# Column dots of a diffusion-transformer layer: where the unused products are written, and new tables for the order of the work

## The chip, the cores and the metric

The kernel runs on one core of a Trainium2 chip, which works with five engines that run side by side, each through its own list of instructions in order: TensorE (PE; PEld is its loading of weights), VectorE (DVE), ScalarE (ACT), GpSimd (POOL) and SyncE (SP). SyncE only starts transfers (DMA) here. The metric is the device time of one launch in microseconds, as a median of several runs.

## The reference

One step of a transformer layer for two groups of 128 tokens (a prompt and a sample), all in float32, with D_MODEL = 2048:

```python
sh1, sc1, g1, sh2, sc2, g2 = split(silu(cond) @ w_ada + b_ada, 6)
h = rms_norm(x, norm1_w) * (1 + sc1) + sh1
qa, ka, va, qb, kb, vb, ga, gb = split(h @ w_in)            # 2048 x 8704
oa = window_attention(qa, ka, va, cache_a, sink)
ob = neighbourhood_attention(qb, kb, vb, cache_b, rpb)
x = x + g1 * ((sigmoid(ga) * (oa @ w_br_a) + sigmoid(gb) * (ob @ w_br_b)) @ w_out)
h2 = rms_norm(x, norm2_w) * (1 + sc2) + sh2
x = x + g2 * (square(relu(h2 @ w_up)) @ w_down)             # 2048 x 8192, 8192 x 2048
```

Here `cond` is one vector for each group, so `silu(cond) @ w_ada` is a product of two rows with a matrix of 2048 x 12288. The outputs are the two results x and the normalised keys and the values of both attentions for the prompt.

## The kernel before

**Weight steps.** The large products are walked through in 456 weight steps, one after another: w_in first (the first 72 steps, then the two gates up to step 135), then the two branch products (136 to 167), w_out (168 to 199), the first part of w_up (200 to 215), and then in turn eight groups of 16 steps of w_down and seven of w_up. A step takes a weight tile of 128x1024 float32 (`raw`, 512 KB, loaded by SyncE) and does 12 matmuls of 128x512. Each float32 product is made of three products of fp32r numbers: the weight is split into a high part `wH`, a copy that ScalarE makes (`copy`, line 103), and a low part `wL` = `raw` - `wH`, which VectorE makes (line 265); the activations are split in the same way (`hH`, `hL`). The three products are wH x hH, wL x hH and wH x hL (lines 323 to 325, 434 to 436). For the steps listed in `LO_DMA`, ScalarE writes -wH (line 271) and a transfer started by GpSimd adds the raw weight to it in place (line 272). In the seven late w_up groups a pair of tiles is combined as in fast matrix multiplication, with further tiles `t` (line 1361), `tH`, `tL`, `uH`, `uL` (line 1373), `XH`, `XL` and `YB`, which VectorE and ScalarE make, and with accumulators `Q` (lines 1295 to 1297).

**The order of the work.** It is written out by hand, and no scheduler changes it: the function `run` walks the steps, and at each step it issues, to all engines, the loads that are due, the high and the low parts that are due, the step's matmuls and then the side work that is listed for this step. How far ahead these are is a matter of tables with one digit for each step: `RUN` (loads), `HIA` (high parts) and `LOOK` (low parts). Other tables name the steps at which side work is issued: `POST` and `JOBS` (attention), `U_AT`, `M_AT`, `P_UP`, `STAT_AT`, `XS_AT`, `CONST_AT`, `ADA_AT`, `ROW_AT`, and, for the dots below, `DOTS1`, `DOTS` and `DOTS2`. The tiles `raw`, `wH`, `wL`, `aT` and most others come from one pool of 54 buffers of 4 KB a partition, each reused when its last reader is done. Some accumulators are seeded: `seed` copies earlier sums into the two PSUM banks on ScalarE (line 103, `acc<-u_kvA` or `acc<-dsum`), so that the step's first matmul must wait for it.

**The column dots.** Most of `silu(cond) @ w_ada` isn't done on TensorE. A tile `aT` of 128x1024 transposed weights is loaded by SyncE (`dot_load`), and for each of the two condition vectors (s = 0 and 1), which lie in `cB` on all partitions, VectorE multiplies the tile with the vector and sums along the row (`dot`, line 1522). The sums go into a column; the products themselves are written somewhere and never read. There are 144 such tiles and so 288 dots. The tables list the step of a tile's first dot; the second is issued one step later. For s = 0 the products go into `junk`, a uint8 tile of which there is one buffer; for s = 1 they go over `aT` itself. Two instructions of VectorE that write the same place are kept in order by a wait of the second one for the first.

The second part of the layer begins with a norm: the residual sums (lines 1067, 1068), square sums on ScalarE (line 1072), a power on GpSimd (line 149), and the scaled rows `h2f` (line 1145), which TensorE transposes (line 1153).

Of the kernel before, what the change touches and what calls it, by code (L numbers as in the profile page):

```python
# [18 lines left out]
P = 128  # L19
# [13 lines left out]
FB_DVE = 0  # L33
FB1 = 12
H_AT = 41
DOTS1 = [16, 17, 17, 19, 21, 27, 28, 32, 33, 34, 34, 38, 38, 38, 40, 40]
CHUNKS = [2, 2, 2, 4, 6]
NFAST = 8
FAST = {1: (0, 1, 2, 3, 4, 5, 6, 7), 2: (0, 1, 2, 3, 4, 5, 6, 7), 3: (0, 1, 2, 3, 4, 5, 6, 7), 4: (0, 1, 2, 3, 4, 5, 6, 7), 5: (0, 1, 2, 3, 4, 5, 6, 7), 6: (0, 1, 2, 3, 4, 5, 6, 7), 7: (0, 1, 2, 3, 4, 5, 6, 7)}
# [14 lines left out]
LOOK = "320122121112425413003123131135113254310254350030712111112489598342112325488911310001241110220222620000300000133400492100202426272442137656655964688684888655653375207130430225548804351610138881841040342174117523461045214446120432245411630040106853042961221010000201202222102552542682111475746010001224011275268574765000072101111321216724428800000406300034322212447772056830563557354369716120300331113174563712714401401033133311121375789630000046530676935775"
RUN = "535358982521111211111000000030102324221111112122111110400652246572543003264232120122432752120112142152010012210035788736651103254942768867787999998987232212799999975115897587998887988775789998987770031443789698865239899876766555766886999623766758875434952511611133325753488988557066786888855675457768777795999985878788788878868488887888988699988672200555565048944929988999999987899999887876245789999999999384555456235656556714366470168961004152442522213555"
CONST_AT = [44, 56, 80, 86, 104, 86]
ADA_AT = [None, 5, 13, 20, 24, 38]
XS_AT = {1: 14, 2: 2, 3: 23}
POST = {('kvA', 0): [54, 57, 78], ('qA', 0): [54, 59, 66], ('qA', 1): [62, 70, 79], ('kB', 0): [71, 71, 79], ('qB', 0): [75, 82, 91], ('kB', 1): [89, 101, 104], ('qB', 1): [82, 87, 106]}
JOBS = [[81, 85, 87, 93, 102], [82, 84, 88, 97, 111], [80, 86, 97, 103, 112], [88, 98, 103, 109, 111], [103, 103, 106, 115, 122], [105, 105, 108, 109, 126], [108, 108, 119, 123, 126], [113, 114, 117, 121, 125]]  # L60
SS_AT = [74, 74, 128, 139]
T_AT = [3, 4]
PREP_IN = [5, 7]
DOTS = [46, 52, 53, 55, 56, 56, 57, 58, 61, 65, 65, 65, 68, 70, 70, 70, 70, 75, 75, 75, 77, 78, 79, 82, 84, 85, 87, 88, 89, 92, 92, 92, 94, 95, 95, 95, 101, 101, 101, 103, 104, 104, 107, 108, 108, 109, 110, 110, 110, 111, 112, 113, 117, 120, 120, 121, 123, 124, 124, 124, 132, 132, 132, 132, 132, 133, 133, 134, 140, 143, 143, 145, 145, 150, 150, 156, 156, 156, 156, 159, 162, 163, 171, 172, 173, 175, 179, 179, 186, 186, 186, 187, 188, 188, 189, 190]
DOTS2 = [235, 237, 238, 264, 269, 270, 301, 301, 330, 331, 333, 361, 367, 371, 393, 397, 424, 425, 428, 433, 433, 433, 433, 433, 439, 439, 441, 441, 441, 442, 444, 444]
STAT_AT = [2, 0, -1, 8]
U_AT = [[[3, 3, 3, 5, 9, 20, 20, 21, 22], [14, 14, 15, 15, 16, 20, 20, 30, 30]], [[2, 5, 5, 5, 16, 16, 18, 29, 29], [11, 13, 14, 14, 14, 26, 26, 27, 27]], [[9, 10, 10, 10, 11, 15, 29, 30, 30], [12, 17, 21, 21, 21, 29, 33, 33, 33]], [[4, 7, 7, 8, 9, 10, 11, 12, 13], [2, 3, 4, 4, 8, 9, 25, 29, 31]], [[0, 4, 4, 10, 10, 21, 21, 23, 24], [3, 3, 5, 5, 9, 24, 30, 31, 31]], [[3, 9, 9, 10, 10, 26, 28, 29, 29], [8, 10, 11, 12, 12, 21, 25, 32, 32]], [[0, 5, 9, 9, 9, 10, 12, 12, 13], [0, 0, 7, 7, 9, 13, 15, 16, 16]]]
XLO_IN = True
STAY = [(3, 1), (3, 2), (5, 2), (5, 3)]
TL_DMA = [2, 3]  # L70
M_TE = (3,)
M_AT = [2, 6, 10]
FLIP = 2
P_UP = [2, 0]
T_UP = [7, 17]
COL = {"qA": 0, "kvA": 1024, "qB": 1536, "kB": 2560, "vB": 3584, "gA": 4608, "gB": 6656}

# [2 lines left out]
def tile_hybrid_step(ctx: ExitStack, tc: tile.TileContext, a):  # L80
# [4 lines left out]
    sp = ctx.enter_context(tc.tile_pool(name="small", bufs=6))  # L85
# [204 lines left out]

    by_dma = sorted(LO_DMA)

    def run():
        loads.sort(key=lambda x: x[:2])
        for st in wsteps:
            while loads and loads[0][0] <= st["i"] + int(RUN[st["i"]]):
                loads.pop(0)[2]()
            for j in sorted(j for j in pre if j <= st["i"]):
                for fn in pre.pop(j):
                    fn()  # L300
            to = st["i"] + int(LOOK[st["i"]]) + 1
            while by_dma and by_dma[0] < to + LO_AHEAD:
# [704 lines left out]
    def br_unit(n):  # L1007
# [503 lines left out]
    def dot(box, job, second, s, tag):  # L1511

        which, fb = job
        if which == "g1":
            dst, part = gcol[which][:, s, fb:fb + 1], 2
        elif which == "g2":
            dst, part = g2col[fb // 4][:, s, fb % 4:fb % 4 + 1], 5
        else:
            nsub, w = which
            dst, part = mod[nsub][w][:, fb, s:s + 1], 3 * nsub + w  # L1520
        out = box["raw"] if s else sp.tile([P, 1024], mybir.dt.uint8, name="junk", tag="J", bufs=1)
        dve.tensor_tensor_reduce(out, box["raw"], cB[s, tag], 1.0, dst if second else baT[:, part, fb:fb + 1],  # L1522
                                 OP.mult, OP.add, dst)

# [94 lines left out]
    for c in range(FB_DVE // 2):  # L1619
        box = {}  # L1620
# [97 lines left out]
```

## Time and profile before

| | |
|---|---|
| median of 3 runs | 1298.91 us (1298.57 to 1299.99) |
| span of the profiled execution | 1296.4 us |
| VectorE, column dots, one each (line 1522) | 1.29 us |
| ScalarE, one copy of 128x1024 (line 103) | 1.04 us |
| transfers | 430.54 MB, mean 332 GB/s |

The profile is of one execution. The span runs from its first to its last instruction; the device time of that execution isn't given apart from the runs, and the median lies 2.5 us above the span. In rows of the profile, line numbers are those of the kernel, `out<-in` names the tiles, and a bracket at the end of a timeline row holds the time that the engine stood idle before it and what ended that. All times are in microseconds from the span's start.

### The profile page before, as it was taken

Reading aid. Unit: us, or ns where it says so; the run is one execution under the profiler, and the core shown is the slowest. Engines: PE = TensorE matmul, PEld = TensorE weight load, DVE = VectorE, ACT = ScalarE, POOL = GpSimd, SP = SyncE. Lnnn points to the kernel's source line nnn. Section 1 sums busy time; section 2 is a strip of 40 time slices with the busy share of each in tenths; the row PEclk is TensorE's granted clock in tenths of the full one; section 3 lists DMA queues with packets and bytes.
Section 4 is the critical chain, followed back from the end, with each engine's and each line's share of the span. In section 5 each row is a group of like instructions: output and inputs, shape, how many; then the busy total and the mean of one; then the engine's idle time right before and its main releaser. Section 6 shows DMA issues by size and latency. Waiting matters only on the chain.

```text
span 1296.4 us, 18038 instructions
## 1 busy us (share of the span) xinstructions
PE 1283.7 (99%) x6074; PEld 1043.7 (81%) x6074; DVE 1215.9 (94%) x1610; ACT 962.4 (74%) x1363; POOL 104.1 (8%) x129
## 2 busy tenths in 40 slices
PE   8999999999999999999999999999999999999998
PEld 4777788888878888888887888888888888888886
DVE  4599999999999999999889999999999999999997
ACT  5535779878676755746798798887899878899872
POOL 0000002121200000001101000100000000010010
PEclk9999999999999999999999999999999999999999
DMA  9999999999999999999799999899999989999995
GB/s 372 408 409 409 394 348 378 355 331 338 363 355 367 381 388 324 343 371 308 252 283 305 327 298 326 283 292 353 296 334 250 299 302 290 309 292 347 379 345 178
DMA packets 158428, 430.54 MB, mean 332 GB/s; under 512 B 53072, under 2 KB 54336, under 8 KB 158336
## 3 DMA queue, kind: packets, MB, share of 16 engines
q1 hardware_dynamic: 145264, 383.39, 80.2%
q0 software_dynamic: 12880, 45.91, 16.6%
q8 instruction: 47, 0.77, 0.2%
q14 instruction: 45, 0.37, 0.1%
q10 hardware_dynamic: 192, 0.10, 0.1%
HBM read 403.35 MB, written 14.99 MB: 323 GB/s over the span
## 4 chain that ended last, share of the span: by engine, by line
PE 80%; DVE 8%; DMA 5%; ACT 5%; issue 2%; POOL 0%; DVEq 0%; SPq 0%; ACTq 0%
PE acc L323 15%; PE acc L324 15%; PE acc L325 15%; PE Q L1296 5%; PE Q L1297 5%; PE Q L1295 5%; PE acc L434 5%; PE acc L436 5%; PE acc L435 5%; DVE wL L265 1%; DMA araw<-in_w_pair 1%; DVE aT L1522 1%; DVE junk L1522 1%; PE ps_ada L340 1%; DMA raw<-in_w_down 1%
## 5 line engine op out<-in xcount | busy, mean ns | idle before, releaser
L103 ACT ACTIVATE wH<-raw 128x1024 fp32r<-128x1024 f32 (+1 forms) x347 | 348.3, 1044 | 129.1 <-DMA raw<-in_w_in 39.5
L265 DVE TENSOR_TENSOR wL<-raw,wH 128x1024 fp32r<-128x1024 f32 x297 | 347.9, 1222 | 6.8 <-ACT wH L103 5.6
L434 PE MATMUL acc<-wH,hH 128*128 128x512 f32 x276 | 108.6, 393 | 0.0
L435 PE MATMUL acc<-wL,hH 128*128 128x512 f32 x276 | 107.5, 390 | 0.0
L436 PE MATMUL acc<-wH,hL 128*128 128x512 f32 x276 | 107.5, 390 | 0.0
L323 PE MATMUL acc<-wH,hH 128*128 128x512 f32 x256 | 102.9, 402 | 0.0
L324 PE MATMUL acc<-wL,hH 128*128 128x512 f32 x256 | 100.1, 391 | 0.3 <-DMA wL<-in_w_in 0.3
L325 PE MATMUL acc<-wH,hL 128*128 128x512 f32 x256 | 99.9, 390 | 0.0
L1522 DVE CUSTOM_DVE_ANT_0 junk<-aT,cB,cols 128x1024 uint8<-128x1024 f32 x72 | 92.6, 1286 | 0.7
L1522 DVE CUSTOM_DVE_ANT_0 aT<-aT,cB,cols 128x1024 f32<-128x1024 f32 x72 | 92.0, 1298 | 0.5
L1361 DVE TENSOR_TENSOR t<-raw 128x1024 f32<-128x1024 f32 x56 | 68.4, 1222 | 2.2 <-PE acc L324 1.3
L103 ACT ACTIVATE uH<-raw 128x1024 fp32r<-128x1024 f32 x56 | 58.9, 1051 | 14.6 <-DVE raw L1367 11.1
L1373 DVE TENSOR_TENSOR tL<-t,tH 128x1024 fp32r<-128x1024 f32 x56 | 68.4, 1222 | 1.0 <-ACT tH L103 0.9
L1373 DVE TENSOR_TENSOR uL<-raw,uH 128x1024 fp32r<-128x1024 f32 x56 | 68.4, 1222 | 0.2
L103 ACT ACTIVATE tH<-t 128x1024 fp32r<-128x1024 f32 x56 | 58.8, 1050 | 11.7 <-DVE t L1361 8.4
L103 ACT ACTIVATE XH<-raw 128x1024 fp32r<-128x1024 f32 x56 | 58.8, 1051 | 10.2 <-PE acc L324 5.3
L434 PEld LDWEIGHTS acc<-wH,hH 128*128 128x128 f32 x276 | 51.8, 188 | 12.4 <-issue 2.1
L436 PEld LDWEIGHTS acc<-wH,hL 128*128 128x128 f32 x276 | 51.8, 188 | 11.0
L435 PEld LDWEIGHTS acc<-wL,hH 128*128 128x128 f32 x276 | 51.8, 188 | 10.7 <-DVE wL L265 0.2
L324 PEld LDWEIGHTS acc<-wL,hH 128*128 128x128 f32 x256 | 48.1, 188 | 11.0 <-DMA wL<-in_w_in 0.9
L323 PEld LDWEIGHTS acc<-wH,hH 128*128 128x128 f32 x256 | 48.1, 188 | 10.0 <-issue 0.7
L325 PEld LDWEIGHTS acc<-wH,hL 128*128 128x128 f32 x256 | 48.1, 188 | 10.0
(668 smaller groups left out, 3468.3 us busy)
## 6 DMA issues: line engine op xcount, KB each, us to landing
raw<-in_w_in SPq DMA_DIRECT2D x133, 512.0 KB, 10.2
raw<-in_w_down SPq DMA_DIRECT2D x128, 512.0 KB, 10.2
raw<-in_w_upF SPq DMA_DIRECT2D x112, 512.0 KB, 6.6
aT<-in_w_adaT SPq DMA_DIRECT2D x80, 512.0 KB, 9.9
aT<-in_w_gT SPq DMA_DIRECT2D x64, 512.0 KB, 10.2
araw<-in_w_pair SPq DMA_DIRECT2D x48, 512.0 KB, 10.2
raw<-in_w_out SPq DMA_DIRECT2D x32, 512.0 KB, 10.1
XL<-in_w_upF POOLq DMA_DIRECT2D x21, 512.0 KB, 8.2
```

Source lines behind the costliest of these rows:

```text
L103: act.activation(out, in_, AF.Copy)
L265: dve.tensor_tensor(st["lo"], st["raw"], st["hi"].bitcast(F32), op=OP.subtract)
L323: pe.matmul(acc[tb], sh, wh[:, k, :], start=f, stop=False, **kw)
L324: pe.matmul(acc[tb], sh, wl[:, k, :], start=False, stop=False, **kw)
L325: pe.matmul(acc[tb], sl, wh[:, k, :], start=False, stop=l, **kw)
L434: pe.matmul(acc[tb], sh, wh[:, k, :], start=kt == 0 and k == 0 and not held and not seeded, stop=False, **kw)
L435: pe.matmul(acc[tb], sh, wl[:, k, :], start=False, stop=False, **kw)
L436: pe.matmul(acc[tb], sl, wh[:, k, :], start=False, stop=last and k == 1 and not hold, **kw)
L1295: pe.matmul(acc, stat[0], hi, start=f, stop=False)
L1361: dve.tensor_tensor(t.rearrange("p (a n) -> p a n", a=2), X.rearrange("p (a n) -> p a n", a=2), Y[:, 0:512].unsqueeze(1).to_broadcast([P, ...
L1373: dve.tensor_tensor(b[n + "L"], v, b[n + "H"].bitcast(F32), op=OP.subtract)
L1522: dve.tensor_tensor_reduce(out, box["raw"], cB[s, tag], 1.0, dst if second else baT[:, part, fb:fb + 1], OP.mult, OP.add, dst)
```

## The change

Line 1521 takes the place for the unused products from `junk` for both dots of a tile, and `junk` now has two buffers in turn. All tables of the side work, and the tables for loads, high parts and low parts, have new numbers. `LO_DMA` has 61 steps where it had 65; of the steps below 200 there are 24 in both. On average a high part is made 7.5 steps ahead of its use (6.4 before) and a low part 5 (4 before), as the order has it.

```diff
-DOTS1 = [16, 17, 17, 19, 21, 27, 28, 32, 33, 34, 34, 38, 38, 38, 40, 40]
+DOTS1 = [17, 18, 19, 20, 23, 27, 30, 32, 34, 34, 37, 37, 37, 38, 40, 40]
...
-HIA = "001212220310102113100001210001100012133414312347213667640200000004600001000320473311554222331525515435463425300014421235010000005113000005420012000010000
...
+HIA = "400113522030440010420200211110041100202342333511313676025142910360060641102322362041732050474443682205452062200032820224629062315003111414070500976030200
...
-ROW_AT = [5, 7, 9, 5]
+ROW_AT = [6, 6, 6, 4]
...
-CONST_AT = [44, 56, 80, 86, 104, 86]
-ADA_AT = [None, 5, 13, 20, 24, 38]
-XS_AT = {1: 14, 2: 2, 3: 23}
+CONST_AT = [48, 54, 79, 82, 103, 89]
+ADA_AT = [None, 5, 13, 21, 24, 38]
+XS_AT = {1: 4, 2: 2, 3: 24}
...
-STAT_AT = [2, 0, -1, 8]
+STAT_AT = [3, 0, -1, 8]
...
-M_AT = [2, 6, 10]
+M_AT = [4, 6, 8]
...
-P_UP = [2, 0]
+P_UP = [3, 1]
...
-        out = box["raw"] if s else sp.tile([P, 1024], mybir.dt.uint8, name="junk", tag="J", bufs=1)
+        out = sp.tile([P, 1024], mybir.dt.uint8, name="junk", tag="J", bufs=2)
```

`LO_DMA`, `LOOK`, `RUN`, `POST`, `JOBS`, `DOTS`, `DOTS2` and `U_AT` change in the same way. What the numbers do is seen in the order of the instructions, at three places.

The first is VectorE among the dots, where w_in is under way, with what each instruction waits for in brackets (DVE_49 is a wait for an earlier instruction of VectorE itself, DMAHW for a transfer; every dot has a second row, the read of its sum). Before:

```order
L1522 ISA junk,scT_158<-aT,cB_1202,cols 128x1024 [waits DMAHW1_49]
L1522 ISA scT_158 128x1
L1522 ISA junk,shT_157<-aT,cB_1202,cols 128x1024 [waits DMAHW2_49,DVE_49]
L1522 ISA shT_157 128x1
L1522 ISA junk,scT_158<-aT,cB_1202,cols 128x1024 [waits DVE_49]
L1522 ISA scT_158 128x1
L1522 ISA aT,scT_158<-aT,cB_1204,cols 128x1024
```

And of the change:

```order
L1522 ISA junk,scT_158<-aT,cB_1085,cols 128x1024
L1522 ISA scT_158 128x1
L1522 ISA junk,shT_157<-aT,cB_1083,cols 128x1024 [waits DMAHW0_49]
L1522 ISA shT_157 128x1
L265 TENSOR_TENSOR wL<-raw,wH 128x1024 [waits DMAHW1_49,DMASW1_49,PE_49]
L265 TENSOR_TENSOR wL<-raw,wH 128x1024 [waits DMAHW6_49,Activation_49]
L1522 ISA junk,shT_157<-aT,cB_1085,cols 128x1024 [waits DVE_49]
```

Before, the second and third dot into `junk` each wait for the dot directly ahead of them. Of the change, the two dots that follow each other write into two buffers and have no such wait, and where a dot waits for VectorE, the instruction that it waits for is at least two dots back. Of the 288 dots, 72 waited for the instruction directly ahead before, and none does now.

The second is ScalarE ahead of the seeds of one unit of w_in (`acc<-u_kvA`, two copies into PSUM) for the step that starts at 183.90 us in the profile of before; the numbers of tiles are kept. Before:

```order
L271 ACTIVATE wL_1777<-wH_1755 128x1024
L103 ACTIVATE wH_1782<-raw_1780 128x1024
L103 ACTIVATE wH_1786<-raw_1784 128x1024
L103 ACTIVATE wH_1790<-raw_1788 128x1024
L103 ACTIVATE acc_1810<-u_kvA0_1602 128x512
L103 ACTIVATE acc_1811<-u_kvA0_1602 128x512
L103 ACTIVATE u_qA1_1842<-acc_1613 128x512
```

And of the change:

```order
L103 ACTIVATE wH_1735<-raw_1733 128x1024
L103 ACTIVATE u_qA0_1807<-acc_1560 128x512
L103 ACTIVATE u_qA0_1807<-acc_1561 128x512
L103 ACTIVATE wH_1820<-raw_1814 128x1024
L103 ACTIVATE acc_1834<-u_kvA0_1637 128x512
L103 ACTIVATE acc_1835<-u_kvA0_1637 128x512
L103 ACTIVATE wH_1840<-raw_1816 128x1024
```

The copy directly ahead of the seeds now is of a tile that stands three loads of 512 KB further back in SyncE's list than the one that stood there before (raw_1788).

The third is VectorE in the second of the late w_up groups, at the tile `tL` that TensorE waits for near 787 us: tL_7476 before, tL_7577 in the change. Before:

```order
L1373 TENSOR_TENSOR uL_7436<-raw_7288,uH_7435 128x1024
L1361 TENSOR_TENSOR t13_7460<-raw_7309,raw_7311 128x1024
L1363 TENSOR_TENSOR YB_7461<-raw_7311,YB_7461 128x512
L1364 TENSOR_TENSOR raw_7311<-t13_7460,raw_7309 128x512
L1353 TENSOR_TENSOR XL_7466<-raw_7309,XH_7368 128x1024
L1367 TENSOR_TENSOR raw_7311<-raw_7311 128x512
L1373 TENSOR_TENSOR tL_7476<-t13_7359,tH_7475 128x1024
L1373 TENSOR_TENSOR uL_7480<-raw_7307,uH_7479 128x1024
```

And of the change:

```order
L1373 TENSOR_TENSOR uL_7554<-raw_7402,uH_7553 128x1024
L1373 TENSOR_TENSOR tL_7577<-t13_7476,tH_7576 128x1024
L1373 TENSOR_TENSOR uL_7581<-raw_7406,uH_7580 128x1024
L1361 TENSOR_TENSOR t13_7590<-raw_7440,raw_7442 128x1024
L1363 TENSOR_TENSOR YB_7591<-raw_7442,YB_7591 128x512
L1364 TENSOR_TENSOR raw_7442<-t13_7590,raw_7440 128x512
L1353 TENSOR_TENSOR XL_7596<-raw_7440,XH_7502 128x1024
L1367 TENSOR_TENSOR raw_7442<-raw_7442 128x512
```

The five instructions that combine the next pair of tiles stood ahead of this `tL` and its `uL`, and stand behind them now.

More of the change, by code (lines that the diff above doesn't have):

```diff
@@ L44 @@
 SEED_N = (1, 2, 3)
-HIA = "001212220310102113100001210001100012133414312347213667640200000004600001000320473311554222331525515435463425300014421235010000005113000005420012000010000000000000000000000021012212665204021532102641311112210323522242361341141053142223200055003214247021257544122343211113683341000145743332210121441325661014430110444887520000000111114340573232253312001013343333222210001001500002230111000224010178677845355300000003423221200315161210000002001124354264556544"
+HIA = "400113522030440010420200211110041100202342333511313676025142910360060641102322362041732050474443682205452062200032820224629062315003111414070500976030200410286111101410103521135315988144422268052013234215110312255442160307562054430203330210545004238042167505321522284902561121152165643251531160042415120233311010195947134000150023303050471204603303006301576353710211000102412202064225021157350095662144463328110022460421202415391110501235501003758335040521"
 JOIN_LO = 0
@@ L48 @@
 LATE = [1, 0, 0]
-ROW_AT = [5, 7, 9, 5]
+ROW_AT = [6, 6, 6, 4]
 DIRECT = (3,)
-LO_DMA = [54, 64, 77, 81, 90, 96, 98, 104, 106, 107, 113, 115, 125, 126, 134, 137, 147, 154, 167, 179, 193, 195, 197, 199, 202, 203, 215, 216, 220, 222, 224, 226, 228, 230, 235, 242, 248, 252, 271, 277, 280, 294, 297, 302, 312, 316, 328, 335, 340, 346, 354, 356, 370, 382, 386, 390, 393, 397, 403, 408, 418, 434, 438, 448, 449]
+LO_DMA = [65, 78, 82, 89, 90, 97, 99, 103, 105, 109, 113, 118, 122, 125, 141, 146, 150, 170, 182, 184, 189, 193, 194, 196, 202, 215, 216, 220, 222, 224, 226, 228, 230, 232, 238, 247, 248, 269, 272, 294, 298, 300, 303, 309, 328, 338, 352, 354, 376, 390, 392, 398, 399, 406, 407, 420, 431, 436, 445, 447, 451]
@@ L52 @@
 LO_AHEAD = 2
-LOOK = "320122121112425413003123131135113254310254350030712111112489598342112325488911310001241110220222620000300000133400492100202426272442137656655964688684888655653375207130430225548804351610138881841040342174117523461045214446120432245411630040106853042961221010000201202222102552542682111475746010001224011275268574765000072101111321216724428800000406300034322212447772056830563557354369716120300331113174563712714401401033133311121375789630000046530676935775"
-RUN = "535358982521111211111000000030102324221111112122111110400652246572543003264232120122432752120112142152010012210035788736651103254942768867787999998987232212799999975115897587998887988775789998987770031443789698865239899876766555766886999623766758875434952511611133325753488988557066786888855675457768777795999985878788788878868488887888988699988672200555565048944929988999999987899999887876245789999999999384555456235656556714366470168961004152442522213555"
@@ L56 @@
-CONST_AT = [44, 56, 80, 86, 104, 86]
-ADA_AT = [None, 5, 13, 20, 24, 38]
-XS_AT = {1: 14, 2: 2, 3: 23}
-POST = {('kvA', 0): [54, 57, 78], ('qA', 0): [54, 59, 66], ('qA', 1): [62, 70, 79], ('kB', 0): [71, 71, 79], ('qB', 0): [75, 82, 91], ('kB', 1): [89, 101, 104], ('qB', 1): [82, 87, 106]}
-JOBS = [[81, 85, 87, 93, 102], [82, 84, 88, 97, 111], [80, 86, 97, 103, 112], [88, 98, 103, 109, 111], [103, 103, 106, 115, 122], [105, 105, 108, 109, 126], [108, 108, 119, 123, 126], [113, 114, 117, 121, 125]]
+LOOK = "201030020035025405142323030245135354011214137362491212041535093423042754859620300402041012313236531311421203443144061246112128187513017476163632564999259773731801465750013661168848661827834090919546344371337434033545002662210234540407562242135206142954500200001023915249624706601633350385477610001204138781468387721002171042202401112872117811005006092419040302377977597925546584031245938350522520100172045570726245100025524210143089095350024456001691233623"
@@ new lines @@
+RUN = "328227518050231121144111709387020728060092362401441523322508028890024905240221262081468056967314124032144123317353846253680271553300344376618737766031351795278993407793148800759894946056577304835177333290979741846228908972957849188464299610895723874271786923016218151989093198696454849962798795657040649968987568790079369692475230790287495994088976030037138588303766904811996927796839679381766599808978599311762855830218718487347417467973408283570633407067"
+CONST_AT = [48, 54, 79, 82, 103, 89]
@@ L61 @@
+ADA_AT = [None, 5, 13, 21, 24, 38]
+XS_AT = {1: 4, 2: 2, 3: 24}
+POST = {('kvA', 0): [62, 66, 75], ('qA', 0): [52, 57, 65], ('qA', 1): [68, 72, 77], ('kB', 0): [68, 77, 82], ('qB', 0): [76, 79, 92], ('kB', 1): [81, 100, 103], ('qB', 1): [80, 95, 100]}
+JOBS = [[82, 85, 88, 94, 104], [85, 85, 86, 95, 114], [79, 89, 94, 105, 113], [88, 97, 105, 106, 112], [105, 105, 108, 111, 126], [105, 105, 107, 111, 125], [106, 107, 119, 125, 126], [114, 114, 118, 121, 125]]
 SS_AT = [74, 74, 128, 139]
@@ L63 @@
 PREP_IN = [5, 7]
-DOTS = [46, 52, 53, 55, 56, 56, 57, 58, 61, 65, 65, 65, 68, 70, 70, 70, 70, 75, 75, 75, 77, 78, 79, 82, 84, 85, 87, 88, 89, 92, 92, 92, 94, 95, 95, 95, 101, 101, 101, 103, 104, 104, 107, 108, 108, 109, 110, 110, 110, 111, 112, 113, 117, 120, 120, 121, 123, 124, 124, 124, 132, 132, 132, 132, 132, 133, 133, 134, 140, 143, 143, 145, 145, 150, 150, 156, 156, 156, 156, 159, 162, 163, 171, 172, 173, 175, 179, 179, 186, 186, 186, 187, 188, 188, 189, 190]
-DOTS2 = [235, 237, 238, 264, 269, 270, 301, 301, 330, 331, 333, 361, 367, 371, 393, 397, 424, 425, 428, 433, 433, 433, 433, 433, 439, 439, 441, 441, 441, 442, 444, 444]
-STAT_AT = [2, 0, -1, 8]
-U_AT = [[[3, 3, 3, 5, 9, 20, 20, 21, 22], [14, 14, 15, 15, 16, 20, 20, 30, 30]], [[2, 5, 5, 5, 16, 16, 18, 29, 29], [11, 13, 14, 14, 14, 26, 26, 27, 27]], [[9, 10, 10, 10, 11, 15, 29, 30, 30], [12, 17, 21, 21, 21, 29, 33, 33, 33]], [[4, 7, 7, 8, 9, 10, 11, 12, 13], [2, 3, 4, 4, 8, 9, 25, 29, 31]], [[0, 4, 4, 10, 10, 21, 21, 23, 24], [3, 3, 5, 5, 9, 24, 30, 31, 31]], [[3, 9, 9, 10, 10, 26, 28, 29, 29], [8, 10, 11, 12, 12, 21, 25, 32, 32]], [[0, 5, 9, 9, 9, 10, 12, 12, 13], [0, 0, 7, 7, 9, 13, 15, 16, 16]]]
+DOTS = [45, 45, 46, 49, 51, 52, 54, 58, 59, 60, 60, 61, 63, 64, 66, 70, 71, 72, 73, 76, 76, 78, 79, 80, 80, 83, 83, 85, 86, 87, 88, 91, 95, 96, 96, 97, 99, 101, 102, 102, 102, 102, 105, 107, 108, 108, 109, 109, 111, 112, 114, 115, 119, 120, 121, 121, 123, 123, 126, 126, 133, 133, 133, 134, 134, 136, 137, 137, 139, 140, 141, 142, 146, 147, 148, 149, 156, 157, 158, 158, 159, 159, 172, 174, 174, 175, 175, 175, 180, 181, 181, 185, 185, 185, 186, 186]
+DOTS2 = [233, 236, 238, 240, 269, 273, 295, 305, 329, 331, 336, 365, 370, 393, 394, 396, 423, 426, 427, 429, 432, 435, 435, 436, 439, 440, 441, 442, 443, 444, 444, 445]
+STAT_AT = [3, 0, -1, 8]
+U_AT = [[[3, 3, 4, 6, 8, 19, 21, 22, 24], [14, 14, 15, 15, 16, 20, 22, 30, 30]], [[2, 2, 7, 11, 16, 18, 20, 29, 30], [6, 13, 13, 13, 14, 25, 26, 30, 30]], [[8, 9, 10, 10, 10, 15, 25, 30, 30], [12, 20, 20, 20, 21, 28, 33, 33, 33]], [[7, 7, 7, 8, 9, 10, 11, 11, 15], [4, 4, 5, 5, 6, 8, 19, 26, 31]], [[-1, 5, 7, 9, 11, 17, 21, 29, 30], [2, 2, 2, 2, 3, 23, 31, 31, 32]], [[-1, 4, 6, 8, 12, 26, 28, 29, 29], [8, 9, 9, 11, 11, 20, 26, 32, 32]], [[0, 3, 9, 9, 9, 11, 11, 11, 12], [0, 0, 5, 9, 9, 13, 13, 14, 16]]]
 XLO_IN = True
```

## Prediction

> **What bounds the kernel now.** I read the page first (busy time, granted clock), then the windows, then TensorE's waits, then the timeline at each wait.
>
> ```profile
> span 1296.4 us, 18038 instructions
> PE 1283.7 (99%) x6074; PEld 1043.7 (81%) x6074; DVE 1215.9 (94%) x1610; ACT 962.4 (74%) x1363; POOL 104.1 (8%) x129
> PEclk9999999999999999999999999999999999999999
> ```
>
> TensorE is busy for 99% of the span and its clock is granted in full everywhere, so its matmuls are the bound. The change leaves their number and shape alone. Only what stands between them can go or come. The 2.5 us between this span and the median of 1298.91 lie outside the span; I leave them as they are and make the sum against 1296.4 + 2.5 = 1298.9, which is also the median.
>
> ```profile
> 96.00:128.00 32.00, 32.00 (x193) 25.23 (x192) 31.43 (x51) 15.30 (x20) 0.00 (x0) 1.00 1.03 409
> 576.00:608.00 32.00, 32.00 (x142) 26.48 (x142) 31.82 (x45) 17.66 (x20) 3.50 (x4) 1.00 1.04 342
> 640.00:672.00 32.00, 32.00 (x142) 26.23 (x141) 27.48 (x38) 28.52 (x33) 2.69 (x3) 1.00 0.80 222
> 704.00:736.00 32.00, 31.19 (x137) 25.28 (x136) 31.66 (x39) 27.66 (x31) 1.77 (x2) 1.00 1.04 365
> ```
>
> The columns behind the stretch and its length are busy time and count of TensorE, its weight loads, VectorE, ScalarE and GpSimd. A full stretch holds 142 matmuls of 128x512 in 32 us, 0.2254 us each. VectorE is as full as TensorE (31.43 and 31.82 of 32) at both ends of the stretch where the column dots run, yet TensorE does not stand still there: VectorE is full because it works ahead, not because it is late. What TensorE does wait for is short:
>
> ```profile
> PE acc L519 <- ACT hH L103: 1.3, 2, 0.9
> PE ps_ada L340 <- DMA araw<-in_w_pair: 1.0, 2, 0.6
> PE Q L1296 <- DVE uL L1373: 0.8, 1, 0.8
> PE ps_h L1153 <- DVE h2f L1145: 0.6, 1, 0.6
> PE acc L323 <- ACT acc L103: 0.5, 1, 0.5
> PE ps_PT L858 <- ACT prob L836: 0.5, 1, 0.5
> PE acc L324 <- DMA wL<-in_w_in: 0.3, 1, 0.3
> PE Q L1296 <- DVE tL L1373: 0.2, 1, 0.2
> ```
>
> The first two rows belong to the first 47 us, where the order of SyncE's loads is the same before and after; they stay. The other six are all that the change can remove. A wait costs a little more than its row says, because TensorE restarts slowly. The seed at 1269 us shows by how much:
>
> ```profile
> 1267.84 1.07 ACT L103 ACTIVATE wH<-raw 128x1024 fp32r<-128x1024 f32 x1 [2.54 <-DMA raw<-in_w_down]
> 1268.81 1.10 ACT L103 ACTIVATE acc<-dsum 128x512 f32<-128x512 f32 x2
> 1268.54 0.39 PE L325 MATMUL acc<-wH,a15L 128*128 128x512 f32 x1
> 1269.45 0.50 PE L323 MATMUL acc<-wH,a14H 128*128 128x512 f32 x1 [0.52 <-ACT acc L103]
> 1269.78 0.39 PE L324 MATMUL acc<-wL,a14H 128*128 128x512 f32 x1
> ```
>
> From 1268.54 to 1269.78 there are 1.24 us where two matmuls take 0.45: the wait of 0.52 costs 0.79, 0.27 more than it shows. These rows also show the mechanism that matters most below: the two copies that seed the accumulators stand behind a weight copy on ScalarE, and that copy waits for a transfer.
>
> **The dots themselves.** Before, the dot of the first row of a pair writes its unused products into one uint8 buffer, and that of the second row writes them over the weight tile.
>
> ```profile
> 599.38 1.28 DVE L1522 CUSTOM_DVE_ANT_0 junk<-aT,cB,shT 128x1024 uint8<-128x1024 f32 x1
> 600.58 0.08 DVE L1522 DVE_READ_ACCUMULATOR2_ANT shT<- 128x1 f32 x1
> 600.70 1.29 DVE L1522 CUSTOM_DVE_ANT_0 junk<-aT,cB,scT 128x1024 uint8<-128x1024 f32 x1
> 601.91 0.08 DVE L1522 DVE_READ_ACCUMULATOR2_ANT scT<- 128x1 f32 x1
> 601.91 1.28 DVE L1522 CUSTOM_DVE_ANT_0 aT<-aT,cB,shT 128x1024 f32<-128x1024 f32 x1
> ```
>
> A dot into junk right behind another starts at 600.70, 0.12 us after the accumulator read began (600.58). The last dot here, into another place, starts together with the read (601.91 and 601.91). So waiting for the instruction directly ahead costs 0.12 us. Of the 288 dots before (two for each of 144 weight tiles), the order has 72 with such a wait; of those after it has none, because with two buffers the writer waited for is two dots back and long done. That is 72 x 0.12 = 8.6 us of VectorE's time. The Trainium skill ("VectorE: DVE Perf Modes", section "The DRAIN you can't avoid") speaks against it: it gives eight copies 13.88 us with a semaphore after each and the same with one at the end, so by it the saving would be 0. The rows above differ from that by 0.12 us a wait, and this measurement decides.
>
> ```profile
> L1522 DVE CUSTOM_DVE_ANT_0 junk<-aT,cB,cols 128x1024 uint8<-128x1024 f32 x72 | 92.6, 1286 | 0.7
> L1522 DVE CUSTOM_DVE_ANT_0 aT<-aT,cB,cols 128x1024 f32<-128x1024 f32 x72 | 92.0, 1298 | 0.5
> L265 DVE TENSOR_TENSOR wL<-raw,wH 128x1024 fp32r<-128x1024 f32 x297 | 347.9, 1222 | 6.8 <-ACT wH L103 5.6
> ```
>
> The place written changes a dot's length by 12 ns at most (1286 against 1298), which I count as nothing. Four weight steps fewer get their low part by DMA, so VectorE gets four subtractions of 1.22 us more, 4.9 us, all behind step 200. None of this is TensorE's time by itself; it counts only where TensorE waits for VectorE.
>
> **The waits, one by one.**
> - Seed at 1269: in the new order it stands behind a load that is due earlier, so the wait goes: -0.8.
> - wL by DMA (0.3) near 323 us, and a shorter one of the same kind 7 us ahead:
>
> ```profile
> 316.25 0.39 PE L323 MATMUL acc<-wH,hH 128*128 128x512 f32 x1
> 316.89 0.39 PE L325 MATMUL acc<-wH,hL 128*128 128x512 f32 x1
> ```
>
> Two matmuls take 0.64 here, 0.19 too much. With 0.3 + 0.27 for the other that is 0.76. Both are steps whose low part comes by DMA, and the last thing that ScalarE waits for ahead of it lies only 52 and 51 matmuls ahead of the use. In the new order these two are gone, and one other has 53: about 0.35 again. -0.4 in all, nothing if the new one is as late as both.
> - prob (0.5): added up with the durations of such rows, some 12 us less of VectorE's work stands ahead of this softmax in the new order, but on ScalarE other copies stand ahead of it as before. I take 0.5 + 0.27: -0.75; nothing, if ScalarE holds it.
> - tL (0.2) at 787 us: the order of VectorE shown above puts this tL five instructions earlier. 0.2 + 0.27: -0.45.
> - uL (0.8) at 708 us stays, although VectorE saves 8.6 us ahead of it.
>
> ```profile
> 627.56 0.69 DVE L1067 TENSOR_TENSOR t<-g,acc 128x512 f32<-128x512 f32 x1 [0.58 <-PE acc L1102]
> 707.31 1.22 DVE L1373 TENSOR_TENSOR uL<-raw,uH 128x1024 fp32r<-128x1024 f32 x1
> ```
>
> At 627.56 VectorE waits for TensorE: whatever it had saved ends here. From this instruction to that uL the order has 94 instructions before and 94 after, of the same kinds, so the uL comes as late again. 0, or -1.05 (0.8 + 0.27) where ScalarE's part between is faster.
> - h2f (0.6) at 620 us: the residual in front of this norm moves ahead of subtractions on VectorE, but a weight copy of a later load stands ahead of its square sum on ScalarE. Between -0.85 (the wait and its restart gone) and +2.5 (the copy waits for its load as long as the one at 1267.84, 2.54); I take 0, since the two pull in opposite directions.
> - Interruptions: in TensorE's order 49 groups of other matmuls stand between weight matmuls before, and 44 after.
>
> ```profile
> 303.76 0.39 PE L325 MATMUL acc<-wH,hL 128*128 128x512 f32 x1
> 303.99 1.03 PE L740 MATMUL ps_qT<-ident,u_qB 128*128 128x128 f32 x8
> 304.78 0.48 PE L323 MATMUL acc<-wH,hH 128*128 128x512 f32 x1
> 305.09 0.40 PE L324 MATMUL acc<-wL,hH 128*128 128x512 f32 x1
> ```
>
> The matmul behind such a group takes 0.31 to the next (304.78 to 305.09) instead of 0.23, and the group's own start is dear by about as much. Five fewer at 0.08 to 0.16: -0.4 to -0.8, I take -0.6.
>
> **What is new.** ScalarE keeps its order, and in the new order weight copies are made further ahead, so more of them wait for a load while seeds stand behind them. The clearest place is the order of ScalarE shown above, ahead of the step that TensorE starts at 183.90:
>
> ```profile
> 179.00 2.95 ACT L103 ACTIVATE wH<-raw 128x1024 fp32r<-128x1024 f32 x3
> 181.84 1.11 ACT L103 ACTIVATE acc<-u_kvA 128x512 f32<-128x512 f32 x2
> 183.90 0.39 PE L434 MATMUL acc<-wH,hH 128*128 128x512 f32 x1
> q1 hardware_dynamic: 1842, 6.28, 96.3%
> raw<-in_w_in SPq DMA_DIRECT2D x10, 512.0 KB, 10.2
> ```
>
> Before, the seeds run at 181.84, 2.06 us ahead of their use. The last two rows are the transfers from 165 to 182 us: 6.28 MB in 17 us, 0.37 MB/us, so a load of 0.524 MB takes 1.3 to 1.4 us. After, the copy ahead of the seeds is of a load three places later on SyncE. The last load of the three copies at 179.00 was there at about 180 (the third copy starts at 180.95); 3 x 1.3 later is 183.8. With 1.06 for the copy and 0.56 for the first seed the matmul starts at 185.4 instead of 183.90: +1.5. Were that load there at 182 already, it would be 0; at the slowest (180.95 + 3 x 1.4) it is +2.9.
>
> SyncE's loads themselves keep their room: counted in the order, the load with the least has 80 matmuls between the release of its buffer and its use, 70 before (18.0 and 15.8 us at 0.2254), both more than the 10.2 us to landing. I count nothing for them.
>
> At other places of this kind (five that I found between 350 and 1250 us, one of them up to 2.4) no row gives the landing. Between 0 and 5 together; I take +1.0, near the lower end, since before a single seed made TensorE wait in this way (the row of 0.5).
>
> Sum: -0.8 - 0.4 - 0.75 - 0.45 - 0.6 + 1.5 + 1.0 = -0.5, from 1298.9 to **1298.4 us**.
>
> **The rivals.**
> - VectorE's saving shows in full: all six waits go (0.8, 0.76, 0.75, 0.45, 1.05 and 0.85, 4.7 together), the interruptions give 0.8, and ScalarE's new places cost between 0 and 2.5: 1293.4 to 1295.9. For it: 8.6 us less on an engine that is full from 96 to 608 us. Against it: TensorE hardly waits in those stretches, and VectorE's wait at 627.56 wipes the saving out. 0.30, with the cases between here and 0.2% below the median.
> - Slower, by one mechanism: seeds and square sums on ScalarE behind copies of loads that are still on their way. The price is copy + seed (1.6 us) plus the load's lateness; it decides where a load lands less than 1.6 us ahead of the use of what stands behind its copy. If it bites at 184 (2.9), at the norm (2.5) and in half of the other 5, the sum is -3.0 + 2.9 + 2.5 + 2.5 = +4.9: 1303.8. 0.20.
> - The change does nothing: VectorE's waits cost nothing that shows, and the new tables win and lose alike: 1298.9. It lies beside my forecast, and the two together have 0.50. The page named above leads here; its share of that is small, 0.05, by the 0.12 us.
>
> **How the numbers follow.** Two runs of this kernel can be told apart from some 0.2%, 2.6 us: faster is below 1296.3, slower above 1301.5. Faster 0.30, the same 0.50, slower 0.20. The range runs from 1294.3, inside the first rival, to 1302.8, inside the second.
>
> **What would show it.** No dot into junk starts 0.12 us after an accumulator read any more, and VectorE's dots sum to less idle time; the wait for uL near 708 stays, that for the seed at 1269 is gone; a wait of some 1.3 us for a seed appears near 184 us. I am wrong if that one is missing and nothing takes its place, or if stretches of TensorE that showed no wait hold more than 142 matmuls in 32 us.

## Result and profile after

| | median | range |
|---|---|---|
| before | 1299.09 us (4 runs) | 1298.57 to 1299.99 |
| changed | 1333.87 us (4 runs) | 1331.53 to 1335.36 |

The ratio is 1.0263, with a 95% interval of 1.0248 to 1.0277: the change makes the kernel slower by 35 us, where 1298.4 was forecast. The page of the changed kernel begins:

```profile
span 1329.8 us, 18102 instructions
PE 1295.6 (97%) x6074; PEld 1046.3 (79%) x6074; DVE 1215.9 (91%) x1614; ACT 959.1 (72%) x1359; POOL 101.5 (8%) x125
...
PEclk9999999999999999998999999999999999999999
```

The work is the same, and VectorE's busy time is 1215.9 us as before: what the dots save is spent on four more subtractions. The time lies in TensorE's waits. Its wait view, with the total, the number and the longest:

```profile
PE acc L1118 <- DMA wL<-in_w_out: 3.4, 2, 2.1
PE acc L324 <- DMA wL<-in_w_in: 2.7, 2, 1.5
PE acc L325 <- DVE a13L L976: 1.9, 1, 1.9
PE Q L1296 <- DVE tL L1373: 1.9, 1, 1.9
PE acc L324 <- DMA wL<-in_w_down: 1.9, 1, 1.9
PE Q L1295 <- ACT dsum L103: 1.7, 2, 1.0
PE Q L1296 <- DVE uL L1373: 1.6, 2, 0.9
PE acc L323 <- DVE g_gA L1010: 1.5, 1, 1.5
PE acc L325 <- DMA a3L<-fTa: 1.3, 1, 1.3
```

`a3L` and `a13L` are low parts of activations for w_down, made by a transfer and by VectorE; `g_gA` is a gate that VectorE multiplies with the sums of a branch product, and `dsum` is ScalarE's copy of sums of w_down. No row is above 3.4 us, and VectorE, ScalarE and transfers are all among the releasers. The rows of the whole view sum to 28 us, where they were 8 before. Most of the rest of the 33 us of span is what follows a wait: 29 waits, where there were 14, have their restart of some 0.27 us each, and some have more behind them. (By the starts of the matmuls, some 3 us more are gaps too short for the view.) The timeline of TensorE at 1240 us shows it:

```profile
1237.72 0.39 PE L324 MATMUL acc<-wL,a13H 128*128 128x512 f32 x1
...
1240.03 0.50 PE L325 MATMUL acc<-wH,a13L 128*128 128x512 f32 x1 [1.92 <-DVE a13L L976]
...
1240.83 0.63 PE L325 MATMUL acc<-wH,a13L 128*128 128x512 f32 x1
...
1241.26 0.63 PE L323 MATMUL acc<-wH,a13H 128*128 128x512 f32 x1
...
1243.82 0.58 PE L323 MATMUL acc<-wH,a13H 128*128 128x512 f32 x1
```

From 1240.83 to 1243.82 the matmuls start every 0.427 us instead of every 0.227: seven of them, 1.4 us more than the wait itself. The same happens behind the waits near 616 and 963 us, 28 slow matmuls more than before in all, 5.6 us. The windows show that it is the clock (the stretch, its length, TensorE's busy time and count, then the granted clock, the busy share of the DMA engines and GB/s):

```profile
616.17:623.00 6.83, 5.60 (x14) 0.50 1.04 283
964.33:967.74 3.41, 3.41 (x10) 0.50 0.70 144
1240.81:1244.22 3.41, 3.41 (x9) 0.50 1.02 408
```

### The profile page after: what moved, and what is told of

Its sections match the earlier page's. It is cut to its first block, busy times and chain, and to the rows that moved or that the text cites. A ratio compares the mean times of both kernels' runs of the same rounds, so it can differ in the third digit from the quotient of the medians.

```text
span 1329.8 us, 18102 instructions
## 1 busy us (share of the span) xinstructions
PE 1295.6 (97%) x6074; PEld 1046.3 (79%) x6074; DVE 1215.9 (91%) x1614; ACT 959.1 (72%) x1359; POOL 101.5 (8%) x125
## 4 chain that ended last, share of the span: by engine, by line
PE 49%; DMA 10%; DVE 9%; issue 8%; ACT 3%; SPq 0%; POOL 0%; DVEq 0%; POOLq 0%; ACTq 0%
PE acc L324 10%; PE acc L323 10%; PE acc L325 10%; PE Q L1296 4%; PE Q L1297 4%; PE Q L1295 4%; DVE junk L1522 2%; DMA raw<-in_w_out 2%; DMA aT<-in_w_adaT 2%; DMA raw<-in_w_down 2%; DVE wL L265 1%; DMA raw<-in_w_br_b 1%; DMA wL<-in_w_out 1%; DMA wL<-in_w_down 1%; DMA wL<-in_w_in 1%
## 5 line engine op out<-in xcount | busy, mean ns | idle before, releaser
L265 DVE TENSOR_TENSOR wL<-raw,wH 128x1024 fp32r<-128x1024 f32 x294 | 344.6, 1219 | 27.1 <-ACT wH L103 16.8
L1522 DVE CUSTOM_DVE_ANT_0 junk<-aT,cB,cols 128x1024 uint8<-128x1024 f32 x144 | 179.1, 1285 | 0.0
L1522 DVE CUSTOM_DVE_ANT_0 junk<-aT,cB,gc_g 128x1024 uint8<-128x1024 f32 x64 | 79.0, 1280 | 0.0
```

The source lines that it names most:

```text
L265: dve.tensor_tensor(st["lo"], st["raw"], st["hi"].bitcast(F32), op=OP.subtract)
```

## Experiments

**The two halves of the change.** The first kernel has the new line alone, the second the new tables alone.

```diff
-        out = box["raw"] if s else sp.tile([P, 1024], mybir.dt.uint8, name="junk", tag="J", bufs=1)
+        out = sp.tile([P, 1024], mybir.dt.uint8, name="junk", tag="J", bufs=2)
```

> The kernel before with the changed line 1521 alone; all tables as before. Theory A (the new tables are what costs the 35 us, the buffers cost nothing): VectorE's 72 waits of 0.12 us go, TensorE's waits stay where they were or shrink; 1295 to 1299 us, none of the waits for wL by DMA near 348, 380, 616 and 620 us. Theory B (writing into one of two small buffers is itself what costs, for instance because a freed VectorE starts loads that collide): 1315 us or more.

Measured: 1296.71 us (11 runs) against 1299.44 for the kernel before (15 runs), ratio 0.9977 (0.9968 to 0.9986). The buffers alone gain 2.7 us. This is the fastest kernel of the study. Its time is inside what theory A gave, and the four waits named there don't occur.

```diff
 (the changed kernel)
-        out = sp.tile([P, 1024], mybir.dt.uint8, name="junk", tag="J", bufs=2)
+        out = box["raw"] if s else sp.tile([P, 1024], mybir.dt.uint8, name="junk", tag="J", bufs=1)
```

> The changed kernel with the old line 1521: all tables new, the old places for the products. Theory A: the tables carry the loss, so 1330 to 1342 us, since VectorE's waits for itself come back (8.6 us of its time, of which a part reaches TensorE). Theory B: 1299 to 1310 us.

Measured: 1340.98 us, ratio 1.0309 (1.0291 to 1.0327). Theory A holds and B falls: the tables cost 42 us with the old line, and the two buffers take 7 of them away.

**The price of the wait between dots.** The kernel before with one junk buffer for all 288 dots:

```diff
-        out = box["raw"] if s else sp.tile([P, 1024], mybir.dt.uint8, name="junk", tag="J", bufs=1)
+        out = sp.tile([P, 1024], mybir.dt.uint8, name="junk", tag="J", bufs=1)
```

> The kernel before with all 288 dots writing into one single junk buffer. In the order 181 dots now stand directly behind another dot and must wait for it, where 72 did before and none with two buffers. At 0.12 us each VectorE loses 21.7 us, 13 more than before. Theory A (the wait costs 0.12 us of VectorE, and VectorE has little room from 96 to 608 us): 1302 to 1312 us, with waits of TensorE for wL and for attention work in that stretch. Theory F (the waits are free for TensorE, since VectorE works ahead): 1298 to 1300 us.

Measured: 1311.77 us, ratio 1.0099 (1.0082 to 1.0116). The busy rows of two buffers (e1) and of one (this kernel), in this order, and one row of the wait view of this kernel:

```profile
PE 1283.9 (99%) x6073; PEld 1044.4 (81%) x6074; DVE 1210.7 (93%) x1610; ACT 962.2 (74%) x1363; POOL 105.7 (8%) x129
```

```profile
PE 1287.7 (98%) x6073; PEld 1044.5 (80%) x6074; DVE 1225.5 (94%) x1610; ACT 962.1 (73%) x1363; POOL 108.0 (8%) x129
```

```profile
PE acc L324 <- DVE wL L265: 5.4, 6, 1.9
```

With the old tables VectorE is busy for 1210.7, 1215.9 and 1225.5 us with 0, 72 and 181 waits, some 0.08 us for each wait, to which 0.04 us of idle time comes that the timeline shows (600.58 + 0.08 to 600.70 in the prediction's rows). So some 0.12 us a wait, which makes 21.7 us of VectorE's time for 181, and the kernel is 15.1 us slower than e1. Theory A holds, and theory F falls: VectorE's work ahead is no cushion of that size.

**Where the new tables lose.** Two mixes, cut at step 205, of which e6 is the other way round:

```diff
 (e5, the changed kernel; LOOK, RUN and LO_DMA as HIA, the late side work as DOTS2)
-HIA = NEW
+HIA = NEW[:205] + OLD[205:]
...
-DOTS2 = NEW
+DOTS2 = OLD
```

> Two buffers; the new tables for the weight steps below 205 (and for attention, the first dots and the branch products), the old ones from there on (late w_up groups, w_down, the gate dots of the second norm). In the changed kernel 14.6 us of the 33.3 are lost up to 620 us, where step 200 begins, and 18.7 behind. Theory C (the losses are many separate places, each a product that the new tables ask for a little too late, and each place costs by itself): 1296.7 + 14.6 = 1311 us, within 4. Theory D (the tables hang together over the whole program, so that any mix is worse than either): 1325 us or more, as with the mix of the preparation tables alone (1363.8).

> The other way round: old tables below step 205, new ones from there on. Theory C: 1296.7 + 18.7 = 1315 us, within 4, and the two mixes' losses add up to that of the changed kernel. Theory D: 1325 us or more.

Measured: 1317.61 and 1315.21 us, so 20.9 and 18.5 over e1, together 39.4, where the whole set costs 37.2. Theory D falls. Cut by place, the losses add up, within some 2 us. The second mix meets theory C's number; the first is 2.6 us above its range, and its profile waits 4.8 us for the transfer at 620 us where the changed kernel's waits 2.1 near 616. Cut by table the losses don't add up:

```diff
 (the changed kernel)
-HIA, LOOK, RUN, LO_DMA = NEW
+HIA, LOOK, RUN, LO_DMA = OLD
```

> The changed kernel with HIA, LOOK, RUN and LO_DMA of the kernel before; the tables of side work and dots stay new. Theory A3 (the tables that set how far ahead weights are made ready carry the loss): 1300 to 1308 us. Theory A4 (the tables of side work carry it): 1325 us or more. Theory A5 (each set fits only the side work that it was found with): 1325 us or more too, with waits at other places than those of the changed kernel.

Measured: 1363.80 us, 30 slower than the changed kernel. A3 falls. A4's number is met as A5's is, but the new side work alone doesn't explain why the old preparation makes it slower still. That, and the waits at other places, speaks for A5. TensorE's wait view of this kernel begins with low parts that come late on VectorE:

```profile
PE acc L324 <- DVE wL L265: 18.2, 7, 5.5
PE ps_S L811 <- ACT T_qA L746: 7.8, 1, 7.8
```

**Is one table the cause?** ScalarE of the changed kernel stands idle for loads far longer than before, 59 us between 400 and 600 us where it was 14, and 150 us in all where it was 86, as added up over its copies. Three kernels test HIA, and one RUN:

```diff
 (e9, the changed kernel)
-HIA = "400113522030440010420200211110041...
+HIA = "200001211010220000210100100000020...
 (e10, the changed kernel)
-HIA = NEW
+HIA = OLD
 (e11, two buffers and old tables)
-HIA = OLD
+HIA = NEW
 (e12, the changed kernel)
-RUN = NEW
+RUN = [min(9, r + 1) for r in NEW]
```

> The changed kernel with every number of HIA halved (rounded down), so that ScalarE's copies of the high parts are issued fewer steps ahead. In the changed kernel ScalarE stands idle 150 us for a load that its next copy needs (86 us before), 59 us of it between 400 and 600 us (14 before). Theory G (ScalarE's list runs too close behind the loads: its copies hold up what stands behind them): that idle time falls below 110 us and the time to 1310-1322 us. Theory H (the copies are not too early; VectorE and TensorE then wait for them): 1335 us or more, with more waits of VectorE for wH than the 16.8 us of the changed kernel.

> The changed kernel with HIA of the kernel before and all else new. Theory G: 1310 to 1325 us, ScalarE's idle time for loads below 110 us. Theory I (HIA fits the other tables of its own set only): 1335 us or more.

> All old tables but HIA, which is new, and two buffers (1296.7 with the old HIA). Theory G: the new HIA alone brings the loss into the old tables, 1310 to 1330 us, with ScalarE's idle time for loads over 110 us. Theory I: some loss too, but without that idle time. If HIA matters little: 1297 to 1302 us.

> The changed kernel with every number of RUN one higher (9 at most): SyncE's loads are issued a step earlier. Theory J (the loads are issued too late, and ScalarE waits for that reason): ScalarE's idle time for loads falls by 20 us or more and the time to 1315-1325 us. Theory K (the loads wait for a buffer of the pool, which comes free when TensorE is done with a step, so an earlier place in SyncE's list changes nothing or takes a buffer from other work): 1330 us or more.

Measured: 1370.51, 1346.98, 1407.38 and 1352.00 us. In e9 the idle time for loads falls from 150 to 85 us, as theory G wanted, but the time rises by 37: H holds, as the first row below shows, VectorE's in e9 (16.8 us in the changed kernel). In e10 the time is theory I's. In e12 the idle time falls to 113, and the time rises by 18, so J falls. K's number is met, but the earlier loads do change something; whether they took a buffer from other work is open. e11 is 77 us above the highest of its theories. The rows behind the first are of e11, TensorE's and, last, one of ScalarE's timeline:

```profile
DVE wL L265 <- ACT wH L103: 47.4, 28, 4.3
```

```profile
PE acc L323 <- ACT acc L103: 15.3, 2, 9.3
...
PE Q L1296 <- DVE tL L1373: 14.6, 7, 4.5
...
PE acc L323 <- DVE g_gA L1010: 5.8, 1, 5.8
```

```profile
1370.63 1.06 ACT L103 ACTIVATE wH<-raw 128x1024 fp32r<-128x1024 f32 x1 [10.00 <-DMA raw<-in_w_down]
```

In e11 my slower rival shows at full strength: with the new HIA and the old rest, seeds (`acc<-...`) stand behind copies whose loads are not there. The copy of the last row waits 10 us for its load, and the seeds behind it make TensorE wait 9.3. But neither of the two tables explains the loss of the changed kernel: HIA, moved either way, made things worse, and less idle time of ScalarE (e9, e10, e12) came with a longer run each time. Whether that idle time costs something by itself is not shown, since each of these edits moved other work too.

**Can single places be mended?** First all transfers of low parts two steps earlier:

```diff
-LO_AHEAD = 2
+LO_AHEAD = 4
```

> The changed kernel with LO_AHEAD = 4 for 2: ScalarE's half of every low part by DMA, and with it GpSimd's transfer, is issued two steps (5.4 us) earlier. In the trace of the changed kernel TensorE stands still for such a transfer five times near 348, 381, 616, 620 and 1150 us, for 10.1 us in all, and runs at half its clock for some matmuls behind two of them (3.5 us more). Theory A1 (these transfers are issued too late by the new tables): the five waits shrink to nothing, 1320 to 1324 us. Theory A2 (the transfers are late because the loads and buffers ahead of them are late): ScalarE waits instead, and the time stays within 4 us of 1334.

Measured: 1373.12 us. Of the five waits those at 348, 381 and 1150 us are gone, as A1 wanted, those at 616 and 620 stay, and new ones of ScalarE (`acc` 7.3 us, `up` 6.6 us) more than eat the gain. A1 falls, and the time is far above A2's as well. Then only the five late ones:

```diff
-            while by_dma and by_dma[0] < to + LO_AHEAD:
-                prep_to(by_dma[0] - LO_AHEAD)
+            while by_dma and by_dma[0] < to + LO_EARLY.get(by_dma[0], LO_AHEAD):
+                prep_to(by_dma[0] - LO_EARLY.get(by_dma[0], LO_AHEAD))
...
+LO_EARLY = {105: 4, 113: 4, 392: 4}
...
-LO_DMA = [..., 189, 193, 194, 196, ...]
+LO_DMA = [..., 189, 196, ...]
```

> The changed kernel with its five late transfers of a low part mended one by one: those of steps 105, 113 and 392 are issued two steps earlier (alone, not all 61 as before), those of steps 193 and 194 are made by VectorE instead. The five waits and the slower clock behind two of them cost 12.7 us in the changed kernel. Theory C (separate places): about 1321 us, with no wait for wL by DMA over 0.5 us left. Theory E (what is mended here comes up elsewhere, since ScalarE keeps its order and the earlier copies now hold up seeds, as in the run with all 61 moved): 1330 us or more.

Measured: 1334.22 us, no gain. All five waits are gone, and so is the slow clock (the mean granted clock of the profile is 1.000 where it was 0.995). Beside the changed kernel's profile TensorE gains 1.2 to 2.3 us at each of the five. It loses more than that within 7 us behind the first and 4.6 us within 20 us behind the two near 620; what it gains at 1150 is gone at 1301 us. The wait view, in which lines below the new one are one higher:

```profile
PE Q L1297 <- DVE tL L1374: 3.5, 4, 1.9
PE ps_S L812 <- DVE oLA L892: 3.4, 1, 3.4
PE acc L1119 <- DVE wL L266: 2.9, 1, 2.9
PE acc L324 <- ACT acc L104: 2.5, 3, 1.7
```

The second row lies at 355 us, 7 us behind the mended wait at 348, and the third at 621 us, at the place of the mended wait at 620. Last, dots alone. In the changed kernel two dots stand directly ahead of the subtraction for which TensorE waits at 1240 us; VectorE's timeline:

```profile
1235.75 0.68 DVE L1408 TENSOR_TENSOR up<-up,Q 128x512 f32<-128x512 f32 x1
1236.34 1.28 DVE L1522 CUSTOM_DVE_ANT_0 junk<-aT,cB,cols 128x1024 uint8<-128x1024 f32 x1
...
1237.55 1.28 DVE L1522 CUSTOM_DVE_ANT_0 junk<-aT,cB,cols 128x1024 uint8<-128x1024 f32 x1
...
1238.75 1.22 DVE L976 TENSOR_TENSOR a13L<-fTa,a13H 128x1024 fp32r<-128x1024 f32 x1
```

The first of the three kernels moves them behind it; the second takes four more dots from ahead of the evacuation at 544 us (`g_gA`, 1.5 us of wait); the third adds one mended transfer to the first.

```diff
 (e13)
-DOTS2 = [..., 394, 396, 423, 426, ...]
+DOTS2 = [..., 394, 396, 425, 426, ...]
 (e14, with that of e13)
-DOTS = [..., 157, 158, 158, 159, 159, 172, ...]
+DOTS = [..., 157, 162, 162, 164, 164, 172, ...]
 (e15, with that of e13)
+LO_EARLY = {392: 3}
```

> The changed kernel with one number of DOTS2 moved from 423 to 425, so that two dots that stand directly ahead of the subtraction a13L on VectorE (2.4 us) stand behind it. In the changed kernel TensorE waits 1.9 us for a13L at 1240 us, and then runs at half its clock for 8 matmuls (1.4 us more). Theory C (separate places): 3.3 us less, 1330 to 1331.5 us. Theory E (given back at the next place, near 1250 to 1310 us): 1333 to 1335 us, with the wait for a13L gone and others longer.

> As e13, and the four numbers 158, 158, 159, 159 of DOTS moved to 162, 162, 164, 164, so that of six dots ahead of the evacuation of the branch sums (L1010, for which TensorE waits 1.5 us at 544 us) two are left between. Theory C: 1.9 us less than e13, 1328 to 1330 us. Theory E: as e13 or slower, the time coming back at the next waits, up to 620 us, where two low parts by DMA are late.

> As e13, and the low part by DMA of step 392 (TensorE waits 1.9 us for it at 1150 us) issued one step earlier. Theory C: 2.2 us less than e13, about 1328.5 us. Theory E: within 1 us of e13.

Measured: 1335.88, 1334.84 and 1334.44 us, ratios 1.0282 (1.0267 to 1.0298), 1.0288 (1.0254 to 1.0323) and 1.0272 (1.0255 to 1.0289): none differs from the changed kernel by more than the intervals. In each the mended waits are gone. In all three a wait for seeds stands some 42 us behind the place of the mended a13L, where the changed kernel has none: 4.24, 3.73 and 3.95 us, more than the 1.92 that were mended. ScalarE and then TensorE in e13:

```profile
1262.21 1.06 ACT L103 ACTIVATE wH<-raw 128x1024 fp32r<-128x1024 f32 x1 [2.18 <-DMA raw<-in_w_down]
1263.18 2.94 ACT L103 ACTIVATE pla<-up 128x1024 uint16<-128x1024 uint16 x3
...
1274.00 2.59 ACT L103 ACTIVATE fTa<-pTa 128x1024 uint16<-128x1024 uint16 x2 [6.88 <-DMA pTa<-pla]
...
1282.83 1.14 ACT L103 ACTIVATE acc<-dsum 128x512 f32<-128x512 f32 x2
```

```profile
1283.51 0.80 PE L323 MATMUL acc<-wH,a14H 128*128 128x512 f32 x1 [4.24 <-ACT acc L103]
```

Read downwards: a copy waits 2.18 us for its load, the planes behind it on ScalarE are made later, their transposing transfer starts and lands later, ScalarE waits 6.88 us for it, and the seeds behind that make TensorE wait 4.24 us. In the changed kernel the same copies of planes and transposes ran with the seeds at 1277.87. The move of a dot also moves its load in SyncE's list, two steps; whether that or the earlier TensorE makes the load at 1262 late was not tried apart. In e14 the time at `g_gA` is given back at once, by a wait of 3.3 us at 550 us for another step of this evacuation (line 1017). Theory C falls in all four kernels, and the times are theory E's to within some 1 us.

One caution on single places: e13 has the order of the changed kernel up to some 1200 us, and yet its profile waits 2.79 and 3.73 us for the transfers near 381 and 616 us, where that of the changed kernel waits 1.52 and 2.14. Such a wait differs by 1 to 2 us from one execution to another, so what one place is worth can't be read from a single profile to better than that.

## Why the prediction was wrong

The mechanism of the line was right. The 72 waits cost some 0.12 us each (e1, e8), and the place written makes no difference. The Trainium skill ("VectorE: DVE Perf Modes", section "The DRAIN you can't avoid") has the semaphores between copies cost nothing. The dots, whose accumulator is read behind them, differ from that by those 0.12 us a wait. What the line is worth was not forecast apart; alone it gives 2.7 us. Two of the prediction's small terms show in e1 already, with the old tables, in one profile of each: the seed at 1269 no longer makes TensorE wait, and the wait for h2f is gone, since VectorE comes to the residual at 614.40, where it was 615.31. Of these 0.9 us TensorE was 0.2 earlier already at 365 us, so the norm gains 0.7. The first row is of the kernel before, the second of e1:

```profile
615.31 0.68 DVE L1067 TENSOR_TENSOR t<-g,acc 128x512 f32<-128x512 f32 x1
614.40 0.68 DVE L1067 TENSOR_TENSOR t<-g,acc 128x512 f32<-128x512 f32 x1
```

So I credited the seed to the new order where it went with the buffers alone, and took 0 for the norm where the buffers alone give -0.7. That uL near 708 stays was right: its 0.8 us of wait are there in e1 as before, although VectorE had 5.2 us less work. tL at 787 and the seed at 1269 are gone in the changed kernel, as said. prob keeps 0.4 of its 0.5 us (-0.75 was wrong), and the two late transfers of low parts made room for five, with 8.0 us of wait, not for one of 0.35 us. That the fewer interruptions gave 0.6 isn't shown.

The step that failed is "What is new", with its two terms of +1.5 and +1.0. The +1.5 does not exist: the copy ahead of the seeds near 184 us waits for its load, as said, but only 0.46 us; it starts at 182.49, not at 183.8, and no wait for these seeds is in the view.

```profile
182.49 1.06 ACT L103 ACTIVATE wH<-raw 128x1024 fp32r<-128x1024 f32 x1 [0.46 <-DMA raw<-in_w_in]
183.45 1.11 ACT L103 ACTIVATE acc<-u_kvA 128x512 f32<-128x512 f32 x2
```

The +1.0, "Between 0 and 5 together", stood for all that I had not looked at, and measured 37 us (the changed kernel against e1), more than the range of any case. I looked for new waits at the places where TensorE had waited before, and at one kind of new place, seeds behind loads on ScalarE. But in the new order each product has a new distance to its use, and the list of VectorE, of ScalarE or of the transfers can bring one too late. Where VectorE was concerned I had checked four places; the waits came for a13L, g_gA and another tL. That VectorE is full from 96 us on was read as working ahead; e8 shows that 21.7 us taken from it make the kernel 15.1 us slower. The slower rival named one mechanism and gave it 1303.8; it exists (e11, e13), but in the changed kernel waits for seeds are 0.6 of the 28 us. And no term held what follows a wait of about 2 us, the slower clock, which is 5.6 us of the 33.

What is shown: the tables carry the loss (e1, e2), and both halves of the program have their part of it (e5, e6). In the four kernels that mended single transfers or dots, other waits took the time back. What stays open is which property of the new set makes it worse as a whole than the old one. Neither table that was tried alone is it (HIA whole, RUN by one step); `LOOK`, `LO_DMA` and the tables of side work were not tried alone. The three mixes by table (e4, e10, e11) were slower than both sets, which speaks for tables that fit only the others of their own set.

## What to carry to other kernels

When a change comes with a new set of tables for an order written by hand, measure the mechanism with the old tables and the tables with the old mechanism first; here the one gained 2.7 us and the other lost 42. TensorE was busy for 99% of the time with the old set, and the few waits seen there did not tell where the new set would wait: forecast such a change with a wide range to the slow side. Mending the new set place by place gained nothing here; whether it can be mended as a whole was not tried.

## What the hardware showed

A wait of about 2 us can slow TensorE's clock to half behind it. In the changed kernel this followed waits of 2.14, 1.92 and 1.92 us (616, 963 and 1240 us), and not one of 1.91 us (1150 us). Where the slow stretches lie tells why. They begin at 616.17, 964.33 and 1240.81 us, which is 102 and 81 times 3.413 us apart, and last 3.41 us or twice that. If the trace is divided into stretches of 3.413 us on this grid, each of the three waits lies whole in the stretch ahead of a slow one (the last, from 1238.11 to 1240.03, in 1237.40 to 1240.81), while the wait at 1150 us is cut at 1148.65 into 0.66 and 1.25 us. All 17 traces, from 60 us on and each divided by its own slow stretches, have 63 stretches at full clock with 1.88 us or more of idle time of TensorE, and half clock follows 61 of them; it follows 2 of the 6144 with less. In e7 a wait of 3.4 us (355 us) is cut into 1.6 and 1.8, and no slow clock follows. So the idle time within one such stretch counts, and not the length of a wait; the limit of 1.9 us is fitted to these traces.

The Trainium skill ("TensorE: Matmul & The Clock Gate", section "HAM oscillation — how this bites in real kernels") warns of idle gaps of more than about 3.4 us. Waits of little more than half of that did it here, so the measurement decides: the price of a 2 us wait is 2.3 us with its restart, or 3.7 with seven slow matmuls behind it. The Trainium skill ("TensorE: Matmul & The Clock Gate", section "Wait — 56ns, not 53.3ns?") has a pitch of 426.7 ns for N = 512 at half clock. The pitch of 0.427 us in the slow stretches agrees.

VectorE starts a dot while the accumulator of the one before is read (601.91 and 601.91 in the prediction's rows), unless it must wait for it; the wait costs some 0.12 us, measured by 0, 72 and 181 of them.
